# Gate and seam units of the adaptive norms as row sums on VectorE, and forward Fourier transforms as rounded products

## The chip, the core and the metric

The kernel runs on one core of a Trainium2 chip. The core has a matrix engine (TensorE, PE in the profile; its weight loads are PEld), a vector engine (VectorE, DVE), a scalar engine (ScalarE, ACT), GpSimd (POOL) and SyncE (SP), which in this kernel mostly issues transfers. Each engine works through its own list of instructions in order; semaphores join them. The metric is the device time of one execution in microseconds (us).

## The reference, cut to what matters

Two layers over 256 latent tokens `h` and 256 context tokens `hc`, of width 1024. Layer 0 mixes tokens with a Conformer convolution, layer 1 with an mLSTM; an MLP of width 4096 follows each. Every sub-layer is scaled, shifted and gated by a map of a vector: latent tokens by `c`, context tokens by `c_ctx`.

```python
def adaln(cvec, w, b):
    return jnp.split(jax.nn.silu(cvec) @ w + b, 6, axis=-1)     # w: 1024 x 6144

def conformer_conv(u, rows, w_pw1, b_pw1, w_dw, b_dw, ln_g, ln_b, w_pw2, b_pw2):
    a = u @ w_pw1 + b_pw1
    a = a[..., :CONV_DIM] * jax.nn.sigmoid(a[..., CONV_DIM:])
    if rows is None:
        a = dwconv(a, w_dw)                                      # context: 31 taps over 256 tokens
    ...
    a = jax.nn.silu(layer_norm(a + b_dw, ln_g, ln_b))
    return a @ w_pw2 + b_pw2

for i in range(DEPTH):
    sh1, sc1, g1, sh2, sc2, g2 = adaln(c[:, None, :], ada_w[i], ada_b[i])
    csh1, csc1, cg1, csh2, csc2, cg2 = adaln(c_ctx, ada_w[i], ada_b[i])
    ...
    h = layer_norm(ALPHA * h + g1 * y, ln1_g[i], ln1_b[i])
    h = layer_norm(ALPHA * h + g2 * sq_relu_mlp(modulate(h, sh2, sc2), ...), ln2_g[i], ln2_b[i])
    # the context stream hc likewise, with csh1 ... cg2, in layer 0
```

## The kernel before

**Products.** A product in full precision is done as three rounded products: each factor is split into a rounded part `wh` (a cast on ACT, line 155) and the rest `wl` (a subtraction on DVE, line 156); PE does lines 186, 189 and 190 for each pair of tiles. Weights come by SP in tiles `raw` of 128x2048 (1 MB), of which there are three buffers. Plain f32 products are used where the operands aren't split.

**The adaLN map.** Its 6144 columns are 12 units of 512: units 0 to 3 are shift and scale of the mixer, 4 and 5 its gate, 6 to 9 shift and scale of the MLP, 10 and 11 the MLP's gate. Layer 0's units 4 to 11 are done in three ways: by PE in blocks (`ada_mm`, line 356: 32 columns holding `c` and `c_ctx`, 128 rows of the map, 512 columns, into the bank `fl`); units 10 and 11 by DVE, which in `gate2_step` adds weight tile times one entry of `c` into `A` for both streams (lines 1081 and 1083), after which `gate2_sums` (line 1087) adds the 128 rows on PE with four products against a column of ones, `hot`; unit 9, called the seam unit here because its eight blocks are placed between the convolution's two halves, by `ada_mm` (`more`, line 1117 on). Layer 1's units are done by `AdaV` on DVE during layer 0's MLP: columns with `tensor_tensor_reduce` (a row sum of weight times a broadcast row `crow`, line 434), and units 4 and 5 (attention's gate, only for the latent stream) by accumulation over `ar` tiles. `AdaV.row` (line 455 on) turns these two accumulators into rows at the start of attention, with a split, four products against ones (line 461) and two additions (line 463).

**Context's convolution** goes through Fourier transforms along the tokens. The gated product E of the first 1x1 convolution is turned by PE (`turn`, line 924) or, for some channels, by way of memory (`vturn3`; a quarter comes back from `a_dr` into `A`). `A` holds 128 tokens x 4 groups x 1024 channels. `fwd` multiplies it with transform matrices (line 948 for the two full groups `tt` 0 and 1, line 953 for 2 and 3) half by half, `h` = 0 and 1 being 512 channels each; groups overlap, so masked copies of the matrix `F0` (`ge32`, `lt32`, `ge96`) stand in. `products` multiplies by the filter (lines 966 and 967, DVE), `back` transforms back (line 978, PE), `token_norm` normalizes over channels, and `silu` turns (line 1141) and activates (line 1144) the result.

**Order.** The order on each engine is the scheduler's. It takes the text's order, dependences and `tc.issue_after(x)`, which holds an instruction behind x. The loop `gemm` calls `pw1_next(m, ...)` after each 128-column tile m of the first 1x1 convolution; the units' steps, the transposes and the loads hang on those calls. The MLP calls `each1(c, m, s)` and `each0(c, m, s)` for chunk c.

Of the kernel before, what the change touches and what calls it, by code (L numbers as in the profile page):

```python
# [71 lines left out]
def hybrid_kernel(ctx: ExitStack, tc: tile.TileContext, xT, vecs_d, taps_d, bdw_d, ada0_w, ada_w, adaT_w, wg_d, pw1a, pw1, pw2, w1_0, w2_0,  # L72
# [340 lines left out]
    class AdaV:  # L413
# [4 lines left out]
        def __init__(self, l, units, streams, rows=()):  # L418
            self.l, self.units, self.streams, self.i, self.acc = l, list(units) + list(rows), streams, 0, []
            self.ncol, self.loads = len(units), []  # L420

        def step(self):
            n, kt = divmod(self.i - len(self.loads), DT)
            if n == len(self.units):
                return
# [3 lines left out]
            if n < self.ncol:  # L429
                b, half = divmod(kt, 2)  # L430
                col = 4 * self.units[n] + b
                for s in self.streams:
                    o = ada[self.l][:, col, s:s + 1]
                    nc.vector.tensor_tensor_reduce(tmp("S") if s == 0 else w, w, crow[s][half], 1.0,
                                                   o if half else V(f"ada_b{self.l}", col),
                                                   op0=ALU.mult, op1=ALU.add, accum_out=o)
                return
            if kt == 0:
                self.acc.append(tmp("S"))
            a, c = self.acc[-1], cs[:, kt, 14 + self.streams[0]:15 + self.streams[0]]  # L440
            if kt == 0:
                nc.vector.tensor_scalar(a, w, c, None, op0=ALU.mult)
            else:
                nc.vector.scalar_tensor_tensor(a, w, c, a, op0=ALU.mult, op1=ALU.add)

        def load(self):
            n, kt = divmod(self.i, DT)
            u = self.units[n]
            w = adp.tile([P, 512], F32, tag="ar", name=nm("ar"), bufs=2)
            nc.sync.dma_start(w, adaT_w[u - 2 * (u > 5), kt // 2, kt % 2] if n < self.ncol  # L450
                              else ada_w[self.l, u, kt // 4, :, kt % 4 * 512:kt % 4 * 512 + 512])
            self.i += 1
            return w

        def row(self, i, dst):

            parts = tmp("E", F32R), tmp("E", F32R)
            split(*parts, self.acc[i])
            ps = psum(("mm", "fl")[i])
            for k, part_ in enumerate(parts):  # L460
                nc.tensor.matmul(ps, ones_r, part_, start=k == 0, stop=k == 1)
            with tc.high_priority(-300):
                nc.vector.tensor_tensor(dst, ps, dst, op=ALU.add)
# [350 lines left out]
    def masked(name, zero):  # L814
        t = padp.tile([P, L], F32, name=name)
        nc.gpsimd.tensor_copy(t, F0)
        for a_, b_ in zero:
            nc.gpsimd.memset(t[a_:b_, :], 0.0)
        return t
# [85 lines left out]
    turns, three = [], []  # L905

    def vturn3(f, a):
# [5 lines left out]
        if m == 1:  # L913
# [3 lines left out]
            if h == 0:  # L917
                with tc.issue_after(loaded[0]):
                    nc.sync.dma_start(A[:, :, 0:2 * P], a_dr[0])

    def turn(f, a):
# [3 lines left out]
        nc.scalar.copy(A[:, :, f * P:(f + 1) * P], tr.rearrange("p (b c) -> p b c", b=4))  # L925
# [1308 lines left out]
```

## Time and profile before

| measure | us |
|---|---|
| median of 3 runs | 1637.28 (1636.73 to 1637.3) |
| profiled execution | 1636.4 |
| its span | 1634.7 |
| first half of the forward transforms | from 68.97 |
| second half | 135.33 to 140.68 |
| attention's gate row on PE | 1173.34 to 1174.75 |

In the profile, lines such as `PE 1624.8 (99%)` are the busy time of an engine and its share of the span; the chain names what ended last at each step; a timeline row gives start, duration, engine, line, operation, tiles and what ended the wait before. Names of tiles are the program's, with buffer numbers left out. A plain f32 product shows as two records, a rounded one as one.

### The profile page before, as it was taken

To read this page: it belongs to the slowest core of one execution; us is meant where nothing else is said; L and a number is where in the kernel's file an instruction comes from. 1 tells how busy PE (TensorE), PEld (TensorE's weight loads), DVE (VectorE), ACT (ScalarE), POOL (GpSimd) and SP (SyncE) were. 2 spreads that over 40 slices of the span, in tenths; PEclk is the share of its full clock that TensorE was granted. 3 is DMA by queue.
4 is the path that set the end of the run, shared out by engine and by line. 5 is a ranking of instruction groups with operands and counts; after the bars stand their busy time and mean duration, and the time that the engine had idled before them with its cause. 6 is when DMAs were issued, how large, how long until landed. Compare 5 with 4: busy or idle time off the path is not lost.

```text
span 1634.7 us, 22791 instructions
## 1 busy us (share of the span) xinstructions
PE 1624.8 (99%) x8758; PEld 1352.7 (83%) x8758; DVE 1071.5 (66%) x2013; ACT 732.9 (45%) x1176; POOL 15.3 (1%) x67
## 2 busy tenths in 40 slices
PE   9999999999999999999999999999999999999998
PEld 6675998888888998877787899888888888878887
DVE  7697896886635877862234643453489876786777
ACT  4314763232324585552223532443478654555453
POOL 0000000000000000000000000000000000000001
PEclk9999999999999999999999999999999999999999
DMA  9766323556523078697563622342556565675552
GB/s 359 257 219 245 104 104 135 172 195 213 174 91 142 23 236 258 199 302 229 194 226 139 248 106 103 130 180 104 177 204 229 209 223 206 235 294 182 181 198 85
DMA packets 88124, 306.87 MB, mean 188 GB/s; under 512 B 12844, under 2 KB 31184, under 8 KB 60112
## 3 DMA queue, kind: packets, MB, share of 16 engines
q1 hardware_dynamic: 65552, 289.12, 50.3%
q10 hardware_dynamic: 22464, 16.30, 3.1%
q8 instruction: 69, 1.13, 0.3%
q14 instruction: 39, 0.32, 0.1%
HBM read 287.52 MB, written 17.86 MB: 187 GB/s over the span
## 4 chain that ended last, share of the span: by engine, by line
PE 98%; DVE 1%; ACT 0%; issue 0%; DVEq 0%
PE mm L186 18%; PE mm L189 18%; PE mm L190 18%; PE mm L202 10%; PE mm L226 3%; PE mm L224 3%; PE mm L225 3%; PE cv L226 2%; PE cv L224 2%; PE cv L225 2%; PE fl L356 1%; PE ln L224 1%; PE ln L225 1%; PE ln L226 1%; PE fl L225 1%; PE fl L224 1%
## 5 line engine op out<-in xcount | busy, mean ns | idle before, releaser
L156 DVE TENSOR_TENSOR wl<-raw,wh 128x1024 fp32r<-128x1024 f32 x344 | 419.0, 1222 | 262.8 <-ACT wh L155 260.4
L155 ACT CAST wh<-raw 128x1024 fp32r<-128x1024 f32 x344 | 359.4, 1053 | 455.2 <-PE mm L189 275.3
L189 PE MATMUL mm<-u,wh 128*128 128x512 f32 (+1 forms) x802 | 288.7, 361 | 0.0
L186 PE MATMUL mm<-u,wh 128*128 128x512 f32 (+1 forms) x674 | 239.4, 356 | 0.0
L190 PE MATMUL mm<-u,wl 128*128 128x512 f32 (+1 forms) x674 | 238.2, 355 | 0.0
L189 PEld LDWEIGHTS mm<-u,wh 128*128 128x128 f32 x802 | 151.2, 189 | 23.0 <-issue 0.8
L186 PEld LDWEIGHTS mm<-u,wh 128*128 128x128 f32 x674 | 127.2, 189 | 20.5 <-issue 2.4
L190 PEld LDWEIGHTS mm<-u,wl 128*128 128x128 f32 x674 | 127.1, 189 | 18.5 <-issue 0.8
L186 PE MATMUL mm<-xm,wh 128*128 128x512 f32 x256 | 100.2, 391 | 0.0
L190 PE MATMUL mm<-xm,wl 128*128 128x512 f32 x256 | 99.6, 389 | 0.0
L186 PE MATMUL mm<-hid,wh 128*128 128x512 f32 (+1 forms) x256 | 93.0, 364 | 0.0
L189 PE MATMUL mm<-hid,wh 128*128 128x512 f32 (+1 forms) x256 | 92.8, 362 | 0.0
L190 PE MATMUL mm<-hid,wl 128*128 128x512 f32 (+1 forms) x256 | 92.7, 362 | 0.0
L224 PE MATMUL mm<-wh,xl 128*128 128x512 f32 x208 | 81.4, 393 | 0.0
L225 PE MATMUL mm<-wh,xl 128*128 128x512 f32 x208 | 81.1, 390 | 0.0
L226 PE MATMUL mm<-wl,xl 128*128 128x512 f32 x208 | 80.9, 392 | 0.0
L189 PE MATMUL mm<-qq,wh 128*128 128x272 f32 x256 | 73.9, 289 | 0.0
L186 PE MATMUL mm<-qq,wh 128*128 128x272 f32 x256 | 73.5, 288 | 0.0
L190 PE MATMUL mm<-qq,wl 128*128 128x272 f32 x256 | 73.5, 288 | 0.0
L1382 DVE SCALAR_TENSOR_TENSOR E<-pad,vecs,E 128x512 f32<-128x512 f32 x64 | 47.9, 748 | 19.3 <-ACT E L1380 18.2
L155 ACT CAST hid<-E 128x256 fp32r<-128x256 f32 (+1 forms) x70 | 34.0, 487 | 58.9 <-DVE E L1223 54.8
L156 DVE TENSOR_TENSOR rr<-mm,rr 128x256 fp32r<-128x256 f32 x64 | 27.0, 422 | 50.8 <-ACT rr L155 50.8
(600 smaller groups left out, 3267.4 us busy)
## 6 DMA issues: line engine op xcount, KB each, us to landing
raw<-w SPq DMA_DIRECT2D x64, 1024.0 KB, 4.8
raw<-wo SPq DMA_DIRECT2D x32, 1024.0 KB, 4.9
raw<-ada_w SPq DMA_DIRECT2D x22, 1024.0 KB, 6.4
ar<-adaT_w SPq DMA_DIRECT2D x64, 256.0 KB, 3.0
raw<-wv SPq DMA_DIRECT2D x16, 1024.0 KB, 6.6
raw<-wq SPq DMA_DIRECT2D x16, 1024.0 KB, 4.8
raw<-wk SPq DMA_DIRECT2D x16, 1024.0 KB, 4.8
u<-wqT SPq DMA_DIRECT2D x56, 256.0 KB, 5.4
```

The costliest lines, as they stand in the source:

```text
L155: c = nc.scalar.copy(hi, src)
L156: lastsub[0] = nc.vector.tensor_tensor(lo, src, hi.bitcast(F32), op=ALU.subtract).ins
L186: a = nc.tensor.matmul(ps, wh, xh, start=start, stop=False)
L189: nc.tensor.matmul(ps, wh, xl, start=False, stop=False)
L190: lastmm[0] = nc.tensor.matmul(ps, wl, xh, start=False, stop=stop).ins
L202: nc.tensor.matmul(o_, w_, x_, start=start and i == 0, stop=stop and i == 15)
L224: nc.tensor.matmul(ps, xh, wh, start=start, stop=False)
L225: nc.tensor.matmul(ps, xl, wh, start=False, stop=False)
L226: return nc.tensor.matmul(ps, xh, wl, start=False, stop=stop).ins
L356: a = mark_unit[0] = nc.tensor.matmul(ps[32 * j:32 * j + 32], cs[:, kt, 14 - 2 * v:46 - 2 * v], blocks[kt], start=first and kt < 4, stop=l ...
L1382: nc.vector.scalar_tensor_tensor(s2_(acc), pad[:, :, k:k + C], V("w_conv", m * QTAP + k), s2_(acc), op0=ALU.mult, op1=ALU.add)
```

## The change

It does five things.

1. **Forward transforms.** For `tt` 0 and 1, `F0` is split into `FH` and `FL`, its masked copies into two rounded parts each (made by DVE from a column of masks `mc`, not by POOL), and these two groups of `A` are split into rounded parts in tiles `u`. Each plain product becomes three rounded ones: 36 products in place of 12. The two other groups stay as they were.
2. **Gate units 10 and 11** of layer 0 leave the convolution; `AdaV` makes them as row sums in the MLP's first chunk (`ada_g2`). The products against `hot` go.
3. **The seam unit 9** becomes 16 row sums on DVE (`unit9_step`) during the first 1x1 convolution, at m 8 to 11; its eight blocks on PE go. The blocks of unit 7 and the loads around them are placed anew.
4. **The row of c** that row sums need is no longer loaded from the host's rows and activated on ACT: `cs` is written to memory `c_dr` by ACT's queue and read back as a broadcast row, into `A` for unit 9 and into `crow` later.
5. **Attention's gate** (units 4 and 5 of layer 1) becomes columns, like the other units; the column is written to memory `g_dr` in the last chunk and read back as a row `G1`. Line 461's products and the two additions go.

On the engines, context's second half of the transforms stands thus. First PE, from the last weight product ahead of it (`mm`), with the blocks of unit 6 and 7 (`fl`), the turn of the last product E (`ln`), and the transform. Before:

```order
L190 MATMUL mm_1125<-u_507,wl_1104 128x512
L356 MATMUL fl_1192<-S_1071,cs 32x512
L356 MATMUL fl_1192<-raw_1190,cs 32x512 x4
L924 MATMUL ln_1203<-ident,E_1160 128x128 x4
L356 MATMUL fl_1192<-u_1229,cs 32x512
L948 MATMUL mm_1250<-A,ge_581 128x512
L948 MATMUL mm_1250<-A,lt_584 128x512
L948 MATMUL mm_1249<-A,tab 128x512
```

and now:

```order
L190 MATMUL mm_1159<-u_507,wl_1140 128x512
L356 MATMUL fl_1227<-S_1107,cs 32x512
L915 MATMUL ln_1234<-ident,E_1191 128x128 x4
L356 MATMUL fl_1227<-F_1260,cs 32x512
L944 MATMUL mm_1285<-u_1099,ge32h 128x512
L944 MATMUL mm_1285<-u_1100,lt32h 128x512
L944 MATMUL mm_1285<-u_1099,ge32l 128x512
L944 MATMUL mm_1285<-u_1101,ge32h 128x512
L944 MATMUL mm_1284<-u_1099,FH 128x512
```

The four blocks from `raw` moved out of this place, and the transform reads `u` (1099 and 1100 the rounded parts of two groups, 1101 and 1102 the rest) in place of `A`. Rows of the other quarters of a block are left out.

Second ACT, at the same place; the `DMA` row is the issue of the load from `a_dr`. Before:

```order
L893 ACTIVATE E_1160<-mm_1124,vecs 128x512
L1053 DMA A<-a_dr_602 128x4x256
L925 COPY A<-ln_1118 128x4x128
L1045 ACT_TABLE_LOAD
L155 CAST wh_1213<-raw_1162 128x1024
L925 COPY A<-ln_1203 128x4x128
```

and now:

```order
L874 ACTIVATE E_1191<-mm_1158,vecs 128x512
L1049 ACT_TABLE_LOAD
L1057 DMA A<-a_dr_611 128x4x256
L155 CAST u_1099<-ln_1148 128x128
L155 CAST wh_1244<-raw_1193 128x1024
L155 CAST u_1099<-A 128x256
L155 CAST wh_1252<-raw_1195 128x1024
L155 CAST u_1100<-A 128x256
L155 CAST u_1100<-ln_1148 128x128
L919 COPY A<-ln_1148 128x2x128
```

The load moved behind the table load, and casts of its data (`u<-A`) stand between the weight casts. Rows that only repeat are left out.

Third DVE, the rows around the last product E. Before:

```order
L897 SCALAR_TENSOR_TENSOR E_1160<-mm_1125,vecs,E_1160 128x512
L156 TENSOR_TENSOR wl_1214<-raw_1162,wh_1213 128x1024
L156 TENSOR_TENSOR wl_1218<-raw_1164,wh_1217 128x1024
L156 TENSOR_TENSOR wl_1222<-raw_1164,wh_1221 128x1024
L966 TENSOR_TENSOR E_1261<-mm_1250,HCS 128x512
```

and now (`ISA` is a row sum, or the reading of its accumulator):

```order
L156 TENSOR_TENSOR wl_1245<-raw_1193,wh_1244 128x1024
L156 TENSOR_TENSOR u_1101<-A,u_1099 128x256
L156 TENSOR_TENSOR u_1101<-ln_1148,u_1099 128x128
L1083 ISA raw_1184,ada_93<-raw_1184,A,ada_93 128x512
L156 TENSOR_TENSOR u_1102<-A,u_1100 128x256
L156 TENSOR_TENSOR u_1102<-ln_1148,u_1100 128x128
L878 SCALAR_TENSOR_TENSOR E_1191<-mm_1159,vecs,E_1191 128x512
L156 TENSOR_TENSOR wl_1249<-raw_1193,wh_1248 128x1024
L156 TENSOR_TENSOR u_1101<-ln_1234,u_1099 128x128
L156 TENSOR_TENSOR wl_1253<-raw_1195,wh_1252 128x1024
L962 TENSOR_TENSOR E_1308<-mm_1285,HCS 128x512
```

The splits of the loaded part of `A` and the unit's last row sum now stand ahead of E, which the turn on PE reads.

The diff, cut to its core:

```diff
-    ge32 = masked("ge32", [(0, 32)])
-    lt32 = masked("lt32", [(32, 64), (64, 128)])
-    ge96 = masked("ge96", [(0, 64), (64, 96)])
-    WIN = [[(F0[0:96, :], 0)], [(ge32, 0), (lt32, 1)], [(ge96, 0), (F0[0:96, :], 1)], [(ge32, 1)]]
+    FH, FL = [padp.tile([P, L], F32R, name=n_) for n_ in ("FH", "FL")]
+    split(FH, FL, F0)
...
+    ge32, ge96, lt32 = [masked(n_, i_) for i_, n_ in enumerate(("ge32", "ge96", "lt32"))]
+    F96 = [FH[0:96, :], FL[0:96, :]]
+    WIN = [[(F96, 0)], [(ge32, 0), (lt32, 1)], [(ge96, 0), (F96, 1)], [(ge32, 1)]]
...
+    def a_split(h):
+        for t in range(2):
+            split(*[a_[t][:, 0:2 * P] for a_ in a_parts(h)], A[:, t, h * 512:h * 512 + 2 * P])
...
     def turn(f, a):
         tr = psum("ln")
         for b in range(4):
             mark["tr"] = nc.tensor.transpose(tr[:, b * P:(b + 1) * P], a[:, b * P:(b + 1) * P], ident).ins
-        nc.scalar.copy(A[:, :, f * P:(f + 1) * P], tr.rearrange("p (b c) -> p b c", b=4))
+        sl = slice(f % 4 * P, f % 4 * P + P)
+        for t in range(2):
+            split(*[a_[t][:, sl] for a_ in a_parts(f // 4)], tr[:, t * P:(t + 1) * P])
+        nc.scalar.copy(A[:, 2:4, f * P:(f + 1) * P], tr[:, 2 * P:4 * P].rearrange("p (b c) -> p b c", b=2))
...
             if tt < 2:
-                w_ = WIN[2 * tt + b]
+                w_ = [(fm[k], a_parts(h)[q][t]) for k, q in ((0, 0), (1, 0), (0, 1)) for fm, t in WIN[2 * tt + b]]
                 for i, (fm, t) in enumerate(w_):
-                    a = nc.tensor.matmul(xfs[b], fm, A[0:fm.shape[0], t, sl], start=i == 0, stop=i == len(w_) - 1)
+                    with tc.issue_after(a.ins) if a else nullcontext():
+                        a = nc.tensor.matmul(xfs[b], fm, t[0:fm.shape[0], :], start=i == 0, stop=i == len(w_) - 1)
...
-    ada_g1, ada_s2 = Ada(0, 4, 2), Ada(0, 6, 6)
+    ada_g1, ada_s2 = Ada(0, 4, 2), Ada(0, 6, 3)
...
-        if 7 <= m <= 10:
-            gate2_step(m - 7)
+        if m == 1:
+            for i in range(2):
+                with tc.issue_after(mark["gate"]):
+                    nc.scalar.dma_start(c_dr[i].rearrange("(k p) -> p k", p=P), cs[:, :, 14 + i])
+        if m == 7:
+            crow.extend([A[:, 2 * i + j, 0:512] for j in range(2)] for i in range(2))
+            with tc.issue_after(loaded[0]):
+                c_rows(crow)
+        if 8 <= m <= 11:
+            unit9_step(m - 8)
...
                 nc.scalar.dma_start(A[:, :, 512:512 + 2 * P], a_dr[1])
+            a_split(1)
...
+    def row_sum(l, col, s, half, w, dump):
+        o = ada[l][:, col, s:s + 1]
+        nc.vector.tensor_tensor_reduce(dump, w, crow[s][half], 1.0, o if half else V(f"ada_b{l}", col),
+                                       op0=ALU.mult, op1=ALU.add, accum_out=o)
...
-    def gate2_sums():
-        for i in range(4):
-            mark_unit[0] = nc.tensor.matmul(ada_s2.ps[32 * i:32 * i + 32, :], hot[:, 6 - i:38 - i], A[:, i, 0:512],
+    def fill_end():
+        ada_mm(ada_s2.ps, second, 1, False, True, range(4, 8))
         ada_s2.sb = tmp("F")
         nc.scalar.copy(ada_s2.sb, ada_s2.ps)
...
-        ada_mm(ada_s2.ps, more, 3, False, False)
...
+    def gate_row():
+        nc.scalar.dma_start(g_dr[0].rearrange("(k p) -> p k", p=P), ada[1][:, 16:24, 1])
+
+    ada_n1, ada_n2 = AdaV(1, range(4), (0, 1)), AdaV(1, (6, 7, 8, 9, 4, 5), (1,), gate_row)
+    ada_g2 = AdaV(0, (10, 11), (0, 1))
...
     def each1(c, m, s):
+        if c == 0 and m > 2:
+            for _ in range(1 if m < 6 else 3):
+                ada_g2.step()
...
-    G1 = rows(qe.tile([P, D], F32, name="G1"), rows_d[0:1])
+    G1 = rows(qe.tile([P, D], F32, name="G1"), g_dr)
     R = rows_tile()
-    for i in range(2):
-        ada_n2.row(i, G1[:, HF[i]])
```

More of the change, by code (lines that the diff above doesn't have):

```diff
@@ L413, in hybrid_kernel, with __init__ @@
     class AdaV:
[L418 to L420 removed]
+        def __init__(self, l, units, streams, done=None):
+            self.l, self.units, self.streams, self.i, self.loads, self.done = l, units, streams, 0, [], done
         def step(self):
@@ L428, in step @@
                 self.loads.append(self.load())
[L429 to L444, printed above, removed]
+            b, half = divmod(kt, 2)
+            for s in self.streams:
+                row_sum(self.l, 4 * self.units[n] + b, s, half, w, tmp("S") if s == 0 else w)
         def load(self):
             n, kt = divmod(self.i, DT)
-            u = self.units[n]
             w = adp.tile([P, 512], F32, tag="ar", name=nm("ar"), bufs=2)
-            nc.sync.dma_start(w, adaT_w[u - 2 * (u > 5), kt // 2, kt % 2] if n < self.ncol
-                              else ada_w[self.l, u, kt // 4, :, kt % 4 * 512:kt % 4 * 512 + 512])
+            nc.sync.dma_start(w, adaT_w[self.units[n], kt // 2, kt % 2])
             self.i += 1
             return w
[L455 to L463, printed above, removed]
     def ad(l, s, which):
```

115 lines of the change are left out of this document (57 added, 58 removed).

## The prediction

> **What bounds the kernel now.** I read the page's head and its chain first, then the waits of TensorE (PE).
>
> ```profile
> span 1634.7 us, 22791 instructions
> PE 1624.8 (99%) x8758; PEld 1352.7 (83%) x8758; DVE 1071.5 (66%) x2013; ACT 732.9 (45%) x1176; POOL 15.3 (1%) x67
> PE 98%; DVE 1%; ACT 0%; issue 0%; DVEq 0%
> PE cv L180 <- DVE ones L139: 1.1, 1, 1.1
> PE fl L461 <- ACT x L1513: 0.2, 1, 0.2
> PE ln L1603 <- DVE E L1587: 0.2, 1, 0.2
> PE fl L356 <- DVE E L690: 0.2, 1, 0.2
> ```
>
> PE is busy 99% of the span, makes up 98% of the chain, and waits for others four times, 1.7 us in all. So an edit counts in two ways only: PE work that it removes, and PE waits that it makes. VectorE (DVE) at 66% and ScalarE (ACT) at 45% count only where one of them falls behind PE. The profiled execution took 1636.4 us, 1.7 beyond its span; the median of the three runs, 1637.28, is 0.9 above it. I make the sum against the profiled execution and set the difference on the median. A change under 0.2% (3.3 us) can't be told from none by a measurement of this kernel.
>
> **PE work that goes.** These are pieces of the chain of waits in order of time, and from the timeline the end of attention's gate row.
>
> ```profile
> 127.84 0.23 PE mm L186
> 135.40 5.35 PE mm L948 x12
> 145.55 4.43 PE fl L356 x40
> 151.00 0.99 PE fl L1087 x8
> 1173.34 0.63 PE L461 MATMUL mm<-E,ones 128*128 128x512 f32 x2
> 1174.18 0.73 PE L461 MATMUL fl<-E,ones 128*128 128x512 f32 x2 [0.22 <-ACT x L1513]
> 1174.75 0.63 PE L224 MATMUL mm<-wh,xl 128*128 128x512 f32 x2
> ```
>
> - Transforms: six plain products (twelve records) take 5.35 us in the half shown, and the first half's group is alike. In their place stand 18 rounded ones; a rounded 128x512 product steps by 0.23 us, so 18 x 0.228 = 4.1 us, 1.25 less a half, 2.5 in both.
> - Seam unit 9: 40 records, twenty blocks, take 4.43 us, 0.22 a block. Eight blocks go: 1.8 us.
> - The sums of the gate units (L1087): 0.99 us.
> - Attention's gate row (L461): from 1173.34 to 1174.75, 1.4 us with its wait.
>
> That makes 6.7 us. I expect about 1 of them in the time, because at each place another engine is late next.
>
> **First half of the transforms, 66 to 75 us.**
>
> ```profile
> 66.50 0.75 DVE L897 SCALAR_TENSOR_TENSOR E<-mm,vecs,E 128x512 f32<-128x512 f32 x1 [2.99 <-PE mm L190]
> 67.38 0.66 PE L924 MATMUL ln<-ident,E 128*128 128x128 f32 x4
> ```
>
> PE reaches the transposes as soon as the gating product E has passed DVE. The split of the loaded part of A and of the transposed parts now stands around it on DVE, in idle time of 2.99 us; I let E come 0.35 us later (an estimate: one 128x256 subtraction, 0.42 us in a row below, is then not covered). The fourth transform needs a bank that DVE's first products free, and PE reaches it earlier: 0.2 us of wait (an estimate). Bounds: all 1.25 gained, or nothing, if two or three more of these subtractions get ahead. I take **0.7 gained**.
>
> **Second half, 125 to 141 us: the gain is eaten here.** In the changed order DVE must split the loaded quarter of A (its load sits on ACT's queue) before it makes the last E, which PE's last transposes read.
>
> ```profile
> 126.06 0.69 ACT L893 ACTIVATE E<-mm,vecs 128x512 f32<-128x512 f32 x1 [7.21 <-PE mm L190]
> 126.19 0.61 ACTq L1053 DMA_DIRECT2D A<-a_dr  x1
> 128.24 1.28 ACT L1045 ACT_TABLE_LOAD   x1
> 129.65 1.99 ACT L155 CAST wh<-raw 128x1024 fp32r<-128x1024 f32 x2
> 132.07 0.75 DVE L897 SCALAR_TENSOR_TENSOR E<-mm,vecs,E 128x512 f32<-128x512 f32 x1 [3.78 <-PE mm L190]
> 132.74 3.48 DVE L156 TENSOR_TENSOR wl<-raw,wh 128x1024 fp32r<-128x1024 f32 x3
> 132.78 1.04 PE L356 MATMUL fl<-raw,cs 128*32 128x512 f32 x8
> 133.75 0.65 PE L924 MATMUL ln<-ident,E 128*128 128x128 f32 x4
> A<-a_dr SPq DMA_DIRECT2D x1, 512.0 KB, 3.7
> A<-a_dr ACTq DMA_DIRECT2D x1, 512.0 KB, 5.9
> L155 ACT CAST hid<-E 128x256 fp32r<-128x256 f32 (+1 forms) x70 | 34.0, 487 | 58.9 <-DVE E L1223 54.8
> L156 DVE TENSOR_TENSOR rr<-mm,rr 128x256 fp32r<-128x256 f32 x64 | 27.0, 422 | 50.8 <-ACT rr L155 50.8
> L434 DVE CUSTOM_DVE_ANT_0 S<-ar,crow,vecs x16: 745/750/753, 260.2 to 349.1; 128x512 f32<-128x512 f32 x16
> ```
>
> Before, DVE had waited 3.78 us for PE when it made E at 132.07, and A's load, issued at 126.19, held up nobody. In the changed order ACT does the sigmoid (0.69), then the table load (1.28) and its warming call, and only then issues the load. With the 0.7 us from the first half that is 126.06 - 0.7 + 0.6 + 1.3 + 0.2 = 127.45. Its landing is the disputed number: 3.7 us for the same transfer in the first half, 5.9 here before. I take 3.7, since the adaLN loads on SP's queue that shared the DMA engines with it here now stand, but for one quarter of unit 7, behind a raw load whose buffer is freed by DVE's last row sum, and that sum stands behind this very landing. So it lands at 131.15. Then follow, one after another: ACT's cast of the first part (0.35) and DVE's subtraction (0.35); DVE's row sum (0.75) beside ACT's weight cast (0.95, half of 1.99); ACT's two casts of the second part (0.55); DVE's two subtractions (0.5); then E at about 133.4, with the transposes at 134.25.
>
> PE could begin them at 132.1: unit 7's first four blocks end at 132.78 before, less 0.7, and the raw blocks that stood between (0.97) are gone. It waits **2.15 us**. Behind the transposes (0.58) and four blocks (1.0) come 18 products (4.1), which pause about 0.75 us: DVE does three weight splits of 1.14 with the two last subtractions between them, so the first products of the inverse, which free a bank, begin at 137.9 instead of 137.35. They end at 134.25 + 0.58 + 1.0 + 4.1 + 0.75 = 140.7, where L948 ended before (135.40 + 5.35 = 140.75). Gained up to here, the first half's 0.7 included: **0**. Each us that the load lands later or earlier moves this by one us, down to the 2.15. With 5.9 it is 2.2 slower. The two bounds on the landing are 2.0, this case's quickest row (an output), and 10.2, the slowest of the neighbourhood; I keep the part from 2.0 to 8.
>
> ```profile
> out<-E SPq DMA_DIRECT2D x2, 256.0 KB, 2.0
> S<-ada_w SPq DMA_DIRECT2D x2, 256.0 KB, 10.2
> ```
>
> **145 to 152 us.** Eight blocks and L1087 go, 2.8 us. Twelve blocks instead of twenty end at 145.55 + 2.66 = 148.2.
>
> ```profile
> 148.02 0.82 ACT L1012 ACTIVATE u<-u,mv 128x512 f32<-128x512 f32 x1 [0.43 <-DVE mv L1004]
> 148.86 1.28 ACT L1144 ACT_TABLE_LOAD   x1
> 150.60 1.02 ACT L1144 ACTIVATE S<-ln,vecs 128x256 f32<-128x256 f32 x2 [0.46 <-PE ln L1141]
> ```
>
> The transposes need the normalized u, ready at 148.84, and the next transposes need the bank that ACT's two activations free. Those can begin when the table is loaded, at 150.14 instead of 150.60. So 0.46 us come forward here; a little more if the earlier reduction helps. Bounds: 0 and 2.8. I take **0.6 gained**.
>
> **Attention, 1173 us.** L461's 1.4 us go, but L224 needs ACT's first cast of xl, which follows the activation of the last bank.
>
> ```profile
> 1173.53 0.60 ACT L1513 ACTIVATE x<-fl 128x512 f32<-128x512 f32 x1
> 1174.03 2.24 ACT L155 CAST xl<-raw 128x256 fp32r<-128x256 f32 x7
> ```
>
> One of seven casts takes 0.32 us, so L224 can't begin before 1174.4, 0.3 ahead of 1174.75. The 0.2 us wait of L1603 should shrink too, since DVE's two additions to the gate row are gone. **0.4 gained** (bounds 0.2 and 1.6).
>
> **What I cost at nothing.** The mask splits lie at the start, in DVE's idle time. The row sums in the convolution's first product (unit 9, sixteen of 0.75 us) take the place of 32 accumulations (TENSOR_SCALAR and SCALAR_TENSOR_TENSOR) of 0.75 at the same place. The small transfers of c and of the gate column are written long before they are read. The gate units' 32 row sums (0.83 each with the accumulator's read) go into the first chunk of the first MLP's products, of which DVE already did part: about 20 us more.
>
> ```profile
> 240.00:260.00 20.00, 20.00 (x113) 17.56 (x113) 9.04 (x14) 8.78 (x15) 0.00 (x0) 1.00 0.19 74
>   DMA ar<-adaT_w: 28.0, 21
> ```
>
> The second fence line is of the row sums before: DVE waited 21 times for one of their loads, 28.0 us in all. In the window of 240 to 260 us DVE (third pair: 9.04 busy) has 11 us free; weight splits run ahead of PE, which in the list above waits for none of them in spite of those 28 us. If that cover goes, rival 3 says what it costs.
>
> **Sum.** 0 - 0.6 - 0.4 = -1.0 us: 1635.4 against the profiled execution, **1636.3** against the median.
>
> **Rivals.**
> 1. The load isn't what ends last: it lands as fast as the quickest row, or the 2.15 us and the 0.75 us of pause go with it. Then -1.0 - 2.9 = -3.9: 1633.4. For it: little else should load at the time, and a row exists at 2.0. Against it: the sums above are one queue behind another. Chance 0.20.
> 2. The load lands late, 8.0 us or more after its issue: the wait at the transposes is then 6.4, the sum -1.0 + 4.3 = +3.3, 1640.6, and more beyond. It decides from 8.0 on. Against it: few loads share the engines there. For it: the 10.2 above. Less is enough if the array runs slower after a long pause, which a row of the opening hints at.
>
> ```profile
> L180 PE MATMUL cv<-ones x24: 275/421/579, 1.1 to 5.9; 128*128 128x128 f32 x24
> L180 PE MATMUL mm<-ones x4: 275/275/377, 7.3 to 7.8; 128*128 128x128 f32 x4
> ```
>
> The same product takes 421 ns in the median at the very start and 275 later. At a landing of 5.9 the pause is 4.35 us, the sum +1.2, and the 18 products at 421/275 their time add 2.2: +3.4, 1640.7. The granted clock reads 1.00 in every window I read, and no pause in this trace is long enough to decide. [...] Chance of this rival 0.09.
> 3. The gate units' row sums hold up DVE in the first chunk. Each load may be waited for at the queue's head, 28.0 / 21 = 1.3 us, so sixteen loads add up to 21 us to the 20 us of work; less the 11 us free, the weight splits behind fall up to 30 us back. Against it: the 28 us before cost PE nothing, so the splits' lead takes most of it. If a quarter is left, +7.5: 1643.8. It decides once the lead is used up. Chance 0.05.
>
> **How the numbers follow.** The forecast 0.66, rivals 0.20, 0.09, 0.05. Its own range is 1634.0 to 1638.5 (landing from 2.9 to 5.9 is 0.8 faster to 2.2 slower, and the bounds of the other places). The range for 8 in 10 goes to 1632.8, below rival 1, and to 1640.2, just short of rivals 2 and 3. Faster by over 0.2%: 0.20; within: 0.66; slower: 0.14.
>
> **What would show it.** After: L944's 18 products stepping by 0.23; a wait of PE's transposes (L915) for DVE's E near 132 to 134 us, of about 2 us, and DVE idle until A's load just ahead of it; no L461, and a wait of PE for ACT's xl at 1173. If that first wait is missing, rival 1 is right; if the granted clock falls behind it, rival 2; if PE waits for wl between 240 and 300 us, rival 3.

## The result and the profile after

| kernel | median us | runs | ratio to before (95%) |
|---|---|---|---|
| before | 1636.92 (1636.12 to 1637.3) | 6 | |
| after | 1645.76 (1643.81 to 1647.04) | 6 | 1.0054 (1.0041 to 1.0067) |

The change made the kernel 8.8 us slower, 0.54%. The time lies 5.6 us above the upper end of the predicted range. The profiled execution took 1646.08 us, with a span of 1644.4. Of the experiments below, one run of e_first took 2299.2 us at a granted clock of 0.65 and is left out of its ratio.

The page's head and the waits of PE come first, of the kernel after. A row of waits names who waited, for whom, then the us in total, the times and the longest.

```profile
span 1644.4 us, 22870 instructions
PE 1622.6 (99%) x8742; PEld 1354.4 (82%) x8742; DVE 1085.8 (66%) x2111; ACT 728.0 (44%) x1181; POOL 12.5 (1%) x57
PE 93%; DVE 3%; DMA 2%; ACT 1%; issue 0%; ACTq 0%; DVEq 0%
PE ln L915 <- DVE E L878: 7.6, 2, 6.0
PE mm L224 <- ACT xl L155: 1.0, 1, 1.0
PE cv L974 <- DVE F L962: 0.5, 1, 0.5
PE mm L944 <- DVE E L963: 0.4, 1, 0.4
```

The engine totals hardly moved. The chain did: PE's share fell from 98% to 93%, and transfers, which had no share, hold 2%. One row of waits carries 7.6 us: twice the transposes (L915) wait for the product E, once for 6.0 us. The prediction expected one such wait, of about 2 us, in the second half. The chain in order of time (start, us, what) shows that the long one is in the first half; five rows under 0.25 us are left out:

```profile
48.64 16.05 DMA a_dr<-res
64.71 5.89 DMA A<-a_dr
70.62 0.41 ACT u L155
71.06 0.96 DVE u L156 x3
72.02 0.20 DVE ge96l L801
72.41 0.19 DVE lt32h L801
72.61 0.20 DVE lt32l L801
72.81 0.67 DVE E L878
73.52 1.11 PE ln L915 x4
```

Read it from the bottom. The transposes wait for E; E stands on DVE behind the splits of the loaded part of `A` and three of the masked parts of `F0` (L801); the first split waits for ACT's cast, the cast for the load of `A`, and the load for the write to `a_dr` that feeds it. That write took 16.05 us. Before, the slowest write to `a_dr` took 11.1. These are the landing times of all ten transfers to and from `a_dr`, eight writes and two loads, first before, then after; the longest is in both the write that the first load waits for:

```profile
DMA to landing us min/median/max: 2.8/5.7/11.1
```

```profile
DMA to landing us min/median/max: 2.7/7.9/16.1
```

So the load was issued 5 us later. The first row is SP's timeline before, the other two ACT's queue and SP's after:

```profile
59.75 0.64 SPq L919 DMA_DIRECT2D A<-a_dr  x1
```

```profile
53.65 3.28 ACTq L1037 DMA_DIRECT2D c_dr<-cs  x2
64.71 0.65 SPq L909 DMA_DIRECT2D A<-a_dr  x1
```

What is new on that queue is the write of `c` (L1037), issued at 53.65, 5 us behind the write to `a_dr` in the chain (48.64). Each of its two transfers moves 4 KB, but scatters 128 x 8 single values of 4 bytes, 1024 pieces. The transfers' packets from 58 to 60 us (packets, MB, share of 16 engines' time) on that queue, before and then after, show them:

```profile
q10 hardware_dynamic: 30, 0.01, 1.7%
```

```profile
q10 hardware_dynamic: 1841, 0.01, 70.3%
```

So 0.01 MB on this queue take 70% of the DMA engines' time in place of 2%. From 60 to 64 us little more than this moves, by the same view of after, and the write to `a_dr` still lands only at 64.7; what holds it then is not shown:

```profile
q10 hardware_dynamic: 102, 0.00, 13.5%
```

In the list of transfers (KB each, us from issue to landing) a write of `c` reads:

```profile
c_dr<-cs ACTq DMA_DIRECT2D x2, 4.0 KB, 13.8
```

Before, the load landed at 59.75 + 3.7 = 63.45, 3.05 us before E was made at 66.50, so the order "split, then E" would have had that much slack. After, it landed at 70.60; the two casts and the subtractions follow, and E begins at 72.72. PE stood for 6.04 us. That is not all of the price. The windows (bounds, length, busy us of PE, PEld, DVE, ACT and POOL with instruction counts, granted clock, DMA share, GB/s) go on:

```profile
70.00:72.00 2.00, 0.00 (x0) 0.00 (x0) 0.94 (x4) 0.98 (x3) 0.00 (x0) 1.00 0.99 400
72.00:74.00 2.00, 0.48 (x2) 0.48 (x3) 1.46 (x6) 0.37 (x1) 0.00 (x0) 0.59 1.04 438
74.00:76.00 2.00, 2.00 (x11) 0.43 (x10) 0.58 (x2) 0.62 (x3) 0.00 (x0) 0.50 0.35 147
76.00:78.00 2.00, 2.00 (x8) 1.29 (x5) 0.00 (x0) 2.00 (x3) 0.00 (x0) 0.50 0.32 45
78.00:80.00 2.00, 2.00 (x8) 1.58 (x7) 0.63 (x2) 0.18 (x1) 0.00 (x0) 0.71 0.89 352
```

In the kernel before, the clock reads 1.00 from 66 to 74 us. Here it falls to 0.50: in windows of 0.1 us it reads 0.74 from 72.3 to 72.4, 0.50 from 72.35 to 72.45, 0.62 from 79.1 to 79.2 and 1.00 from 79.2 to 79.3, so 6.8 us at half clock.

The next table is made by matching PE's instructions in two traces: the start in the kernel named, less the start in before, the median of ten-us pieces, in us. The last column is the difference of the spans. The two middle kernels are experiments below.

| kernel | 60 | 100 | 140 | 150 | 160 | 300 | 1100 | 1260 | end |
|---|---|---|---|---|---|---|---|---|---|
| after | 0.0 | 8.0 | 8.5 | 8.0 | 8.6 | 8.9 | 9.9 | 8.7 | 9.7 |
| c_wide | 0.4 | -0.1 | 0.2 | -0.4 | 0.3 | 0.6 | 1.1 | -0.1 | 1.5 |
| no_round | 0.4 | 0.4 | -0.4 | -1.0 | -0.4 | 0.0 | 0.6 | 1.6 | 1.5 |
| gate_only | 0.0 | 0.0 | 0.0 | 0.1 | 0.1 | 0.0 | 1.2 | 0.0 | 0.3 |

The first row says where the time is: 8.0 of the 9.7 us arise between 60 and 100, at the first half of the transforms. Everything else the change does adds up to 1.7 in this execution.

### The profile page after: what moved, and what is told of

It reads as the page before. It is cut to its first block, busy times and chain, and to the rows that moved or that the text cites. A ratio compares the mean times of both kernels' runs of the same rounds, so it can differ in the third digit from the quotient of the medians.

```text
span 1644.4 us, 22870 instructions
## 1 busy us (share of the span) xinstructions
PE 1622.6 (99%) x8742; PEld 1354.4 (82%) x8742; DVE 1085.8 (66%) x2111; ACT 728.0 (44%) x1181; POOL 12.5 (1%) x57
## 4 chain that ended last, share of the span: by engine, by line
PE 93%; DVE 3%; DMA 2%; ACT 1%; issue 0%; ACTq 0%; DVEq 0%
PE mm L186 17%; PE mm L190 17%; PE mm L189 17%; PE mm L202 9%; PE mm L224 4%; PE mm L226 4%; PE mm L225 4%; PE cv L226 2%; PE cv L224 2%; PE cv L225 2%; DMA a_dr<-res 1%; PE fl L356 1%; PE fl L224 1%; PE fl L225 1%; PE fl L226 1%; PE ln L186 1%
## 5 line engine op out<-in xcount | busy, mean ns | idle before, releaser
L224 PE MATMUL mm<-wh,xl 128*128 128x512 f32 x208 | 81.6, 394 | 1.0 <-ACT xl L155 1.0
L186 PE MATMUL mm<-qq,wh 128*128 128x272 f32 x256 | 73.5, 288 | 0.0
L190 PE MATMUL mm<-qq,wl 128*128 128x272 f32 x256 | 73.5, 288 | 0.0
```

The source lines that it names most:

```text
L186: a = nc.tensor.matmul(ps, wh, xh, start=start, stop=False)
L190: lastmm[0] = nc.tensor.matmul(ps, wl, xh, start=False, stop=stop).ins
L224: nc.tensor.matmul(ps, xh, wh, start=start, stop=False)
```

## The experiments

The theory (W): the 4-byte writes of `c` delay other transfers, and the load of `A`, on which E now hangs, is the one that matters. The rivals were that the order on DVE alone makes the wait (O), and that the pause is due to something else in the change.

**c_late: the writes of c at another place.** Same writes, issued in a later call of `pw1_next`.

```diff
-        if m == 1:
+        if m == 4:
             for i in range(2):
                 with tc.issue_after(mark["gate"]):
                     nc.scalar.dma_start(c_dr[i].rearrange("(k p) -> p k", p=P), cs[:, :, 14 + i])
```

> The changed kernel with the two writes of c to memory issued three tiles later (m 4 in place of m 1), so that the writes of A's quarter are alone on ACT's queue. Theory W (the small writes of c hold up the last packets of A's writes): A's first load is issued near 59.8 us again instead of 64.7 and lands by 64.5; PE's wait of 6.0 us for E and the fall of the granted clock near 73 us are gone; the second half still waits 1 to 2 us. Time 8.0 to 9.0 us under the changed kernel's: about 1637. Theory O (it is the order on DVE, with a load that is late for other reasons): A's load stays at 64 us or later and the time stays within 2 us of 1645.8.

Measured: 1641.28 us, ratio 1.0031 (1.002 to 1.0042). The load of `A` was issued at 60.09, and the wait of 6.0 us was gone. But the writes, now issued at 61.94, met the next load of weights. This is its landing in the list of transfers, the longest wait of PE, and two windows, all of c_late:

```profile
raw<-pw SPq DMA_DIRECT2D x1, 1024.0 KB, 11.8
```

```profile
PE cv L974 <- DVE F L963: 2.3, 1, 2.3
```

```profile
82.00:84.00 2.00, 2.00 (x8) 0.29 (x4) 0.70 (x1) 0.00 (x0) 0.00 (x0) 0.70 0.17 29
84.00:86.00 2.00, 2.00 (x6) 1.50 (x5) 1.39 (x2) 0.00 (x0) 0.00 (x0) 0.50 0.87 332
```

Such a load took 4.7 us in before. Its data came late to DVE, PE paused 2.3 us in the inverse transform, and the clock was at half again, by these windows and the next (0.95 from 86 to 88) from 82.8 to 86.2 us. The cause moved with the writes, to another victim; the time that I expected, that of no delay at all, was wrong.

**c_wide: the same bytes in wide pieces.** The column is copied to a tile that is contiguous in each partition, and written as 32 bytes a partition; the host orders the rows of the map to match.

```diff
+            ccol = con.tile([P, 2, DT], F32, name="ccol")
             for i in range(2):
+                nc.vector.tensor_copy(ccol[:, i, :], cs[:, :, 14 + i])
                 with tc.issue_after(mark["gate"]):
-                    nc.scalar.dma_start(c_dr[i].rearrange("(k p) -> p k", p=P), cs[:, :, 14 + i])
+                    nc.scalar.dma_start(c_dr[i].rearrange("(p k) -> p k", p=P), ccol[:, i, :])
```

> The changed kernel with c written at the same place, but as 32 bytes per partition (128 pieces a write in place of 1024 of 4 bytes); the rows of the map's turned weights are permuted to match. Theory W, if it is the number of pieces: A's load is issued near 60 us, time about 1637 as with the writes moved. Theory W, if any small write behind A's writes does it: A's load is late as before, time about 1645. Theory O: no change, 1645.

Measured: 1637.08 us, ratio 1.0002 (0.9993 to 1.0011). The whole loss is gone. The write in the list of transfers, the issue of the load, and PE's longest wait, of c_wide:

```profile
c_dr<-ccol ACTq DMA_DIRECT2D x2, 4.0 KB, 6.5
```

```profile
60.86 0.65 SPq L909 DMA_DIRECT2D A<-a_dr  x1
```

```profile
PE ln L915 <- DVE E L878: 1.4, 1, 1.4
```

The order on DVE is still "split, then E", and it costs nothing there: E began at 67.11 and PE did not wait for it. Rival (O) falls as a cause of its own. The 1.4 us left are the second half's, the forecast one. So this kernel is the change with its one fault taken out, and it shows what the rest is worth: nothing that can be told from none.

**before_c and before_cw: the writes alone, in the kernel before.** The first adds the 4-byte writes of `c` to before, the second the 32-byte ones. Nothing reads them.

```diff
+        if m == 1:
+            c_dr = dp.tile([2, D], F32, name="c_dr")
+            for i in range(2):
+                with tc.issue_after(mark["gate"]):
+                    nc.scalar.dma_start(c_dr[i].rearrange("(k p) -> p k", p=P), cs[:, :, 14 + i])
```

> The kernel before with the two writes of c to memory added at the place where the change has them; nothing reads them. Theory W: A's load is issued 4 to 6 us later than 59.75 and lands 3 to 7 us later; PE's first transform (68.97) waits 0 to 3 us; time 0 to 3 us over the kernel before. Theory O: A's load stays near 59.8 us, time as before within 0.5 us.

> The kernel before with c written to memory at the place where the change does it, unread, as 128 pieces of 32 bytes a write. Theory W: A's load is issued 0 to 1.5 us later than 59.75 (7 us later with 4-byte pieces), PE's first transform doesn't wait, time within 0.5 us of the kernel before. Rival (a second pair of writes behind A's delays them whatever its pieces): issued 5 us or more later, and a wait of 1 us or more.

Measured: 1638.26 us, ratio 1.001 (1.0001 to 1.002), with 4 bytes; 1636.94, ratio 1.0 (0.9991 to 1.0009), with 32. The issue of the load in each, and the wait that only the first has:

```profile
66.81 0.65 SPq L919 DMA_DIRECT2D A<-a_dr  x1
PE mm L948 <- DMA A<-a_dr: 1.3, 1, 1.3
```

```profile
60.70 0.65 SPq L919 DMA_DIRECT2D A<-a_dr  x1
```

The delay of the load is there without any other part of the change, 7 us against 1, and costs 1.5 us. Before, the load fed the transform itself, several us behind E; the change made E wait for it too. The 32-byte writes delay it by 1 us and cost nothing. Two things together made the 8 us: a load that comes late, and an order that puts the product all others hang on behind it.

**e_first: the order of DVE undone, the writes left.** `a_split(0)` moves behind the last E.

```diff
-                a_split(0)
...
         if f == 3:
+            a_split(0)
```

> The changed kernel with the first half's split of the loaded quarter of A written behind the last E, which moves E ahead of it on DVE; the writes of c stay. Theory W: A's load is still issued at 64.7 and lands at 70.6, so E is made near 66.5, the transposes and blocks run at once, and PE waits for the split parts only, 2 to 2.5 us near 69, with the granted clock at 1.00; time 6 to 7.5 us under the changed kernel's, 1638 to 1640. Theory O: the whole wait goes, time near 1636.5.

Measured: 1641.33 us, ratio 1.0028 (1.0016 to 1.0039), more than expected. The transposes no longer waited, but the transform did. The row of PE's timeline ends with its wait; three windows of one us follow:

```profile
71.76 0.80 PE L944 MATMUL mm<-u,ge32h 128*128 128x512 f32 x1 [2.54 <-ACT u L155]
```

```profile
71.00:72.00 1.00, 0.24 (x1) 0.24 (x1) 1.00 (x3) 0.71 (x3) 0.00 (x0) 0.64 1.04 434
72.00:73.00 1.00, 1.00 (x3) 0.57 (x4) 0.33 (x2) 0.57 (x2) 0.00 (x0) 0.50 0.99 418
78.00:79.00 1.00, 1.00 (x5) 0.58 (x4) 1.00 (x2) 0.00 (x0) 0.00 (x0) 0.94 0.00 0
```

After a pause of 2.54 us the clock was at 0.50; by the first window it had fallen at 71.3, 2.1 us after the pause began, and by the last it was back at 78.1, 6.8 us later (0.50 also from 73 to 74 and from 76 to 78). I had expected it to stay at 1.00; that is the miss.

**after_warm: the pause filled.** 36 products whose result nothing uses stand ahead of the first half's last transposes, to keep PE busy through the wait.

```diff
         tr = psum("ln")
+        if f == 3:
+            idle(tr, 36)
```

> The changed kernel with 36 products of ones by ones (128x128, 0.15 us each when the clock is full, 5.4 us in all) ahead of the first half's last transposes; the transposes overwrite what they leave. They fill PE's wait of 6.0 us for E and can't shorten it. Theory K (the wait costs its length and, behind it, 5.6 us at half clock, some 2.8 us): the granted clock stays at 1.00, time 2.5 to 3.5 us under the changed kernel's, about 1643. Without K: time as the changed kernel, 1645.8, or more.

Measured: 1645.04 us, ratio 1.0051 (1.0037 to 1.0064): 0.7 us less than after, where some 3 were expected. The fillers took 0.23 us each, not 0.15 (an estimate: four transposes of that shape took 67.38 to 67.97 in before), and so were longer than the pause that they filled; their row (two records a product):

```profile
67.45 8.30 PE L180 MATMUL ln<-ones 128*128 128x128 f32 x72
```

The transposes now begin at 75.59, 2 us later than the 73.52 of the kernel after. The clock did not fall: the profiled run's mean is 0.999, as in before (after: 0.996), and the first products of the transform step by 0.23 us, in after by 0.43. That gives the price of the fall: from the start of the transposes to that of the inverse transform (L974, here L976) it took 75.59 to 81.84, 6.25 us, against 73.52 to 82.37, 8.85 us, in the kernel after. Half clock cost **2.6 us** there. In the kernel before the same stretch took 67.38 to 74.32, 6.94 us, so the rounded products save 0.69. With the pause of 6.04 this is 6.04 + 2.6 - 0.69 = 7.95 of the 8.0 found.

**a1_sp and e_both: what bounds the second half.** Both start from c_wide. a1_sp puts the second load of `A` on SP's queue, without the hold:

```diff
-            with tc.issue_after(mark["gate"]):
-                nc.scalar.dma_start(A[:, :, 512:512 + 2 * P], a_dr[1])
+            nc.sync.dma_start(A[:, :, 512:512 + 2 * P], a_dr[1])
```

e_both is a1_sp with the splits of both halves behind the last E, as in e_first.

> The changed kernel with c's writes of 32 bytes, and A's load of the second half issued on SP's queue as soon as its writes have landed, in place of ACT's queue behind the last sigmoid. Theory P (in the second half too, E waits behind the split of this load): the load is issued near 122 in place of 126.1 us, PE's wait of 1.4 us for E near 134 goes, and the time falls 1.0 to 1.5 us under that of the kernel with 32-byte writes alone (1637.1): 1635.6 to 1636.1. Rival: the row sums and weight splits ahead of E on DVE hold it as long; wait and time stay within 0.4 us.

> As the kernel with 32-byte writes and the second half's load on SP's queue, and in both halves the split of the loaded quarter of A is written behind the last E, so that E stands ahead of it on DVE. Theory P': what holds E in the second half is the order on ACT and DVE (weight casts, row sums and splits ahead of E), not the landing. Then PE's wait of 1.9 us for E near 134 shrinks under 0.5; the row sums and splits that now stand behind E hold the products back by 0.4 to 1.0 us; time 0.5 to 1.4 us under that kernel's 1637.6. Rival: the work on DVE between 125 and 140 us is the bound whatever its order; the wait moves to the products, and the time stays within 0.4 us of 1637.6.

Measured: 1637.64 us, ratio 1.0005 (0.9996 to 1.0014), and 1637.49, ratio 1.0002 (0.9993 to 1.0011). In a1_sp the load was issued at 122.29, 4 us earlier than in c_wide, and landed at 126.2, 5 us earlier; E still held the transposes for 1.86 us. These are rows of ACT and DVE ahead of E, others left out:

```profile
128.03 2.95 ACT L155 CAST wh<-raw 128x1024 fp32r<-128x1024 f32 x3
130.88 0.71 ACT L155 CAST u<-A 128x256 fp32r<-128x256 f32 x2
129.11 1.23 DVE L156 TENSOR_TENSOR wl<-raw,wh 128x1024 fp32r<-128x1024 f32 x1 [4.89 <-ACT wh L155]
131.32 0.42 DVE L156 TENSOR_TENSOR u<-A,u 128x256 fp32r<-128x256 f32 x1 [0.31 <-ACT u L155]
133.07 0.74 DVE L1084 CUSTOM_DVE_ANT_0 raw<-raw,A,ada 128x512 f32<-128x512 f32 x1
133.74 0.74 DVE L878 SCALAR_TENSOR_TENSOR E<-mm,vecs,E 128x512 f32<-128x512 f32 x1
```

ACT casts the loaded data only at 130.88, behind three weight casts; in c_wide it cast the first part at 131.19, as the load landed, behind two. DVE stood idle for 4.89 us, until the first of these casts. From 131.32 on it has no idle time: two more row sums of 0.75 us (one in c_wide) stand among the splits, and E comes behind them, at 133.74 (133.42 in c_wide). So the earlier load came with another order on ACT and DVE, and that order, not the load, ends last in a1_sp. With the splits behind E (e_both) the wait was 1.06 us, yet the first product with the filter (L962, here L963), which frees a bank for PE, began at 138.45 instead of 138.20, since the splits now come later. How much of this is the order and how much the amount of work on DVE these two do not separate.

**pw2_late: two weight splits taken out of DVE's way.** e_both, with the subtractions for one pair of weight tiles held behind a later group's products.

```diff
+            with tc.issue_after(mark["pr", 2]):
+                lastsub[0] = nc.vector.tensor_tensor(lo, raw[:, m * 1024:(m + 1) * 1024], hi.bitcast(F32), op=ALU.subtract).ins
```

> The kernel with E ahead in both halves, and with the two weight splits of the second pair of tiles of the next product (subtractions of 1.15 us on DVE) held until the products of the third group, near 151 us, in place of standing ahead of the first products near 136. Theory D (DVE's own work between 128 and 141 us is the bound of the second half): the first products begin 2 us earlier, near 136.5, PE's wait of 0.5 us before the fourth transform goes, and 0.5 to 1.5 us are gained by 141; behind 150 the splits delay DVE's next subtractions by up to 1.2 us and take some of it back; time 0.3 to 1.2 us under 1637.5. Rival (the stretch behind, from the statistics to the activations, takes all of it back): within 0.3 us of 1637.5, with longer waits of PE between 148 and 162.

Measured: 1638.38 us, ratio 1.0007 (0.9998 to 1.0016). The first product with the filter began 1.3 us earlier, at 137.12 against 138.45. But the raw buffer came free later, and with it the next load: PE waited 1.79 us for it up to 150.96, after 1.23 us for DVE's normalized u up to 148.07, and the clock read 0.50 from 150 to 156.8 (0.81 in the window from 156 to 158). The gain was given back.

**unit9_pe: the seam unit's row sums back on PE.** c_wide, without `unit9_step` and the row that it reads, with the unit's eight blocks (`more`) between the halves as before.

```diff
-        if 8 <= m <= 11:
-            unit9_step(m - 8)
...
+        ada_mm(ada_s2.ps, more, 3, False, False)
```

> The kernel with 32-byte writes, with one part of the change undone: the seam unit 9 is done by eight blocks on PE behind the second half again (1.8 us of PE work), with no row sums on DVE in the first product and no broadcast of c into A. Theory S (PE waits at the seam for other engines, so these blocks cost nothing there, while the row sums crowd DVE ahead of E): PE's wait for E near 134 us falls under the 1.4 us with the row sums, PE's waits between 148 and 152 us (0.4 and 0.5) go, and the time is 0 to 1 us under 1637.1. Rival (the blocks' 1.8 us were gained in full): 1.5 to 2 us over 1637.1.

Measured: 1638.28 us, ratio 1.0009 (1.0 to 1.0018). The second half's wait for E is gone, and the transforms end at 138.91 against 140.68 before: 1.8 us gained. Three things differ from c_wide there: the row sums are gone from DVE, the load of `A` was issued at 120.36 in place of 126.09, and ACT cast its first part at 128.35, ahead of two weight casts. By a1_sp the early load alone does not do it; which of the other two does was not separated. The gain did not last either, for the blocks' own load came late; the wait and the windows behind it, of unit9_pe:

```profile
PE fl L356 <- DMA raw<-ada_w: 1.9, 1, 1.9
```

```profile
150.00:152.00 2.00, 2.00 (x12) 0.44 (x8) 0.00 (x0) 0.00 (x0) 0.00 (x0) 0.53 1.03 426
152.00:154.00 2.00, 2.00 (x16) 0.44 (x8) 0.00 (x0) 0.78 (x2) 0.00 (x0) 0.62 1.04 406
```

**no_round: are the rounded products worth anything?** c_wide with the plain transforms of before.

```diff
-                w_ = [(fm[k], a_parts(h)[q][t]) for k, q in ((0, 0), (1, 0), (0, 1)) for fm, t in WIN[2 * tt + b]]
+                w_ = WIN[2 * tt + b]
```

> The changed kernel with c's writes of 32 bytes and with the transforms of before (plain f32 products, masked copies, no split of A); the rest of the change stays. It costs 1.25 us of products in each half and takes the splits off ACT and DVE. By my walk through the queues the first half loses 0.5 to 0.7 us, the second gains 0 to 0.5 since E no longer waits: time 0 to 0.7 us over 1637.1. Rival (the rounded products' 2.5 us arrive in full): 2 to 2.5 us over it, 1639.3. Rival (the splits cost more than the products save): under 1636.5.

Measured: 1637.94 us, ratio 1.0006 (0.9997 to 1.0015). In the table above the plain version gains nothing in the first half, where the rounded one gains 0.5, but 0.8 in the second, where the rounded one loses 0.3. At 150 us it stands 0.6 ahead, and a wait of 1.4 us for a weight split at 1229 takes it back. By the median the two can't be told apart.

**gate_only: attention's gate alone, in the kernel before.**

```diff
-    ada_n1, ada_n2 = AdaV(1, range(4), (0, 1)), AdaV(1, range(6, 10), (1,), (4, 5))
+    ada_n1, ada_n2 = AdaV(1, range(4), (0, 1)), AdaV(1, (6, 7, 8, 9, 4, 5), (1,), gate_row)
...
+    g_dr = dp.tile([1, D], F32, name="g_dr")
+    def gate_row():
+        nc.scalar.dma_start(g_dr[0].rearrange("(k p) -> p k", p=P), ada[1][:, 16:24, 1])
...
-    G1 = rows(qe.tile([P, D], F32, name="G1"), rows_d[0:1])
+    G1 = rows(qe.tile([P, D], F32, name="G1"), g_dr)
...
-    for i in range(2):
-        ada_n2.row(i, G1[:, HF[i]])
```

> The kernel before with one part of the change alone: attention's gate (units 4 and 5 of layer 1) as row sums and columns, written to memory and read back as a row; no products with ones and no additions at the start of attention. From the shift between the traces around 1180 to 1240 us (1.0 us forward in the kernel with 32-byte writes): 0.5 to 1.1 us under the kernel before. Rival (PE waits there for ACT's casts as long as the products lasted): within 0.3 us of it.

Measured: 1636.4 us, ratio 0.9998 (0.999 to 1.0007). In the trace it gains 1.2 us between 1140 and 1260, but 1.2 us had been lost between 440 and 460, of which the recorded waits show 0.2. The rest of that loss stays unexplained.

None of these kernels is faster than before by more than its interval.

## Why the prediction failed, step by step

**The step that failed** stands under what I cost at nothing: "The small transfers of c and of the gate column are written long before they are read." I asked when their data is needed, and not what they do to the others meanwhile. 2 x 1024 pieces of 4 bytes took 14 us to land and stretched the write that the load of `A` waits for from 11.1 to 16.1 us. c_wide, which makes the pieces larger and fewer (and adds two small copies on DVE), takes 8.7 us off; before_c shows the same delay without the rest, and before_cw almost none. The gate column's write, 1024 pieces of 4 bytes too, took 10.3 us in after, and c_wide and gate_only, which both have it, are no slower than before. So such a write costs by what waits beside it.

The list of transfers would not have shown it, since before has no such write; but the diff did, with its `"(k p) -> p k"`, which takes the column's values one by one. The packets show about as many pieces: under 512 bytes, from 55 to 76 us, before has 402, after 2445, which is 2043 more for 2048 values of 4 bytes, and c_wide 702, 300 more for 256 pieces of 32 bytes.

**The first half, "0.7 gained".** I put the split of the loaded part "in idle time of 2.99 us" on DVE, and left out that it waits for a load. Its slack was 3.05 us, one subtraction from rows already quoted; a delay of 7.15 used it up. Without the delay the size came near, in part by luck: c_wide gains 0.5. Its 18 products took 4.69 us in place of 5.35, a gap of 0.24 ahead of the fourth transform included, so they save 0.66, where 1.25 less 0.2 was forecast; and E came 0.15 us later behind the products, not 0.35. One term put at nothing was misplaced too: the mask splits do not lie "at the start", but in part right ahead of E (L801 in the chain above).

**Rival 2** described the mechanism (late load, pause, clock), with +3.4 us, but for the second half's load. In the first half it came to 8.0. Its point on the clock held: in the kernel after PE stood from 67.5 to 73.5, and the granted clock fell to 0.50 at 72.4, 4.9 us after the pause began, and was back at 79.2. A shorter pause sufficed in e_first: 2.54 us, with the fall at 71.3, where PE had been busy until about 69.2. The forecast let its own pause of 2.15 us, in the second half, cost no clock, a term that no run shows; that pause came to 1.56 us in the kernel after, up to 142.53, and the clock read 1.00 from 141 to 149.

**The second half, "0".** The wait at the transposes was 1.56 us in the kernel after (2.15 forecast), the pause inside the products 0.44 (0.75). From 100 to 140 the table gives a loss of 0.5 in the kernel after and 0.3 in c_wide, against the forecast 0.7. The size is near, in part by luck. The load's issue did not wait for the table load ordered ahead of it, as ACT's rows after show:

```profile
134.25 0.60 ACTq L1057 DMA_DIRECT2D A<-a_dr  x1
134.78 1.28 ACT L1049 ACT_TABLE_LOAD   x1
```

So it went out 0.2 us behind the start of the sigmoid (134.09), not 2.1, but landed in 5.2 us, not in 3.7: the two misses nearly cancel. Behind the landing the forecast chain is there, and E comes 2.3 us after it, as forecast. Rows of the chain that ended last, after, with DVE's other splits left out:

```profile
134.25 5.22 DMA A<-a_dr
139.49 0.42 ACT u L155
140.56 0.66 DVE raw L1083
141.81 0.66 DVE E L878
```

The step "each us that the load lands later or earlier moves this by one us" was wrong on the earlier side: in a1_sp the load lands 5 us earlier than in c_wide, and PE waits 1.86 us in place of 1.40.

**145 to 152 us, "0.6 gained".** Measured 0.5 at 150 in the kernel after and 0.6 in c_wide. By 160 it is lost again. The inverse at L974 waits 0.5 us for DVE's last product (F, L962), which comes no earlier than before: another engine was next there too, and the prediction stopped at 152.

**Attention, "0.4 gained".** PE waits for ACT's `xl`, as forecast (1.0 us at L224), and the gain by 1260 is 1.2 us in the kernel after: right, and sized too small.

**The first MLP**, rival 3: PE has no wait for weights between 240 and 300. Between 300 and 1100 the kernel after loses 0.9 and c_wide 0.4; where from was not tested.

**What held throughout**: of the PE work removed almost nothing reaches the time. It was also less than the 6.7 us of the sum: PE's busy time is 1621.1 us in c_wide and 1624.8 before, 3.7 less. With the fault out (c_wide) the change gives +0.3 us by the medians, where -1.0 was forecast; and pw2_late and unit9_pe show it once more: each takes away the wait that ends last and meets the next one some 10 us later.

## What to carry to other kernels

- Cost a transfer by its pieces, not its bytes, and ask what it does to its neighbours: 8 KB in 2048 pieces of 4 bytes cost 8 us in the changed kernel, about 4 in its other order (e_first against c_wide) and 1.5 in the kernel before; the same 8 KB in pieces of 32 bytes cost nothing that could be measured.
- When an instruction that waits for a load is put ahead of one on the path, on the same engine (E on DVE: at 72.72 behind the splits in after, at 66.68 ahead of them in e_first), subtract the two times: the load's landing from the moment the path needs the engine. Whatever delays the load by more than that slack is paid for.
- A pause of PE can cost more than its length: here 2.6 us on top of 6.0, at a granted clock of 0.50 (after against after_warm).

## What the runs showed of the hardware

- With pauses of 6.0 us (after), 2.5 (e_first), 2.3 (c_late) and 1.9 (unit9_pe) the granted clock fell to 0.50, during the pause in the first two and 1.2 and 0.3 us behind it in the others; with those of 1.9 (a1_sp, 1.00 from 132 to 142), 1.4 (c_wide, 1.00 from 131 to 143) and 1.3 us (before_c, 1.00 from 68 to 80) it did not. In pw2_late the clock fell in the second of two pauses, 1.2 and 1.8 us, 1.1 us apart. Half clock lasted 6.8 us in after (72.4 to 79.2), e_first (71.3 to 78.1) and pw2_late (150.0 to 156.8), and 3.4 us in c_late (82.8 to 86.2) and unit9_pe (150.1 to 153.5). The length of the pause alone doesn't decide (1.87 us in unit9_pe, 1.86 in a1_sp); what does was not tested.
- Writes in 4-byte pieces lengthened a neighbour on the same queue (11.1 to 16.1 us) and one on SP's queue (a weight load, 4.7 in before to 11.8 us in c_late). Whether the number of pieces or their size does it was not separated.
- The issue of a transfer from ACT's queue ran 0.5 us ahead of the table load that stands before it in ACT's order (134.25 and 134.78 in after).
